# Attention stage of a decoder layer: transpositions at the head of a period, stream units dealt by estimated work

## The chip, the cores and the metric

The kernel runs on one core of one Trainium2 chip. The metric is the device time of one execution in microseconds (us): the median of 3 runs before the change is 1649.64 us (1649.29 to 1649.93). Beside these runs one execution was taken with the hardware profiler. Engines: PE is the matrix engine (PEld its weight loads), DVE the vector engine, ACT the activation engine, POOL the general-purpose vector engine, SP the engine that issues most DMAs.

## The reference

One layer over 512 positions and 2048 channels. Only the attention part matters here; the sentences below say where it stands.

```python
h = rms_norm(x, norm_g[l])
proj = h @ w_in[l]
q, kv, g_logits, z_a, uv, z_b, merge_logits = jnp.split(proj, SPLIT_IDX, axis=-1)
...
ss = jnp.einsum('bqgrd,bgqnkd->bgrqnk', qb, ks).astype(jnp.float32) * scale
...
p_s = jax.nn.softmax(ss.reshape(b, A_KV_GROUPS, A_REP, Q_BLOCK, n_top * SEL_BLOCK), axis=-1)
...
o_s = jnp.einsum('bgrqnk,bgqnkd->bqgrd', p_s.astype(vs.dtype), vs)
...
p_w = jax.nn.softmax(sw, axis=-1)
o_w = jnp.einsum('bgrqk,bkgd->bqgrd', p_w.astype(vwb.dtype), vwb)
o = (gb[:, :, 0, :, :, None] * o_c + gb[:, :, 1, :, :, None] * o_s +
     gb[:, :, 2, :, :, None] * o_w)
```

There are 16 heads of 64 channels in 4 groups, and three branches: a compressed one (o_c, 31 block keys), a selected one (o_s, where all 8 blocks of 64 keys are among the 16 to select, so that it is causal attention) and a window of 512 keys (o_w). Their outputs are gated, summed, and multiplied by SiLU of z_a. The other parts are a chunked gating unit, two up-projections, an output projection and a gated embedding, with the weight matrices read once.

## The kernel before

**The stream.** Every large matrix product is a job in one list (add_job), and a generator, gemm (line 170), works through it. A raw weight tile comes by DMA from SP, ACT casts its high part (hi, line 98), DVE subtracts to get the low part (lo, line 104), and PE multiplies in three matmuls of 512 columns (act_h by hi, act_l by hi, act_h by lo; lines 190 to 192). One `yield` of the generator after such a triple is a **unit**. A cast and a subtraction of 128x512 serve four units; they are issued two to three such tiles ahead (split_to). fill(n) takes n units. At the end of a job its evacuation runs: evac_q (line 277) makes two 64x512 casts and two subtractions of a scaled q tile qs, evac_za (line 292) a tanh and a gating multiply.

**The attention stage** runs while the stream goes through the jobs z0 q2 q3 z1 q4 q5 z2 q6 q7 z3 z4 z5 z6 z7 (za and q of pairs of heads), 16 units each, 224 in all; 19 are taken before its loop. The stage has 48 **slots** (line 748): for each of 8 pairs of heads ft, six slots (ft, i, br), with query block i = 3, 3, 2, 2, 1, 0 and one branch (selected or window) in the first four, both in the last two. A slot goes through four steps:

- scores (line 751): for two heads, two matmuls each of the query block with (i+1) x 128 keys (times branches) into a bank ps_s; DVE adds the position bias and takes the minimum while it moves the result to a tile prob (line 767). The exponentials on ACT (line 776) are issued two flushes later.
- weigh (line 781): DVE takes the reciprocal of the sums (line 785), multiplies by the gates (787) and scales prob (791).
- transpose_probs (line 806), for one block of at most two key blocks: 4 (or 2) transpositions on PE into a bank ps_t, a cast pth on ACT at once, and a subtraction ptl on DVE that is **deferred**.
- values (line 822), for one block: matmuls of pth and ptl with the values into ps_o; with the last block of a 256-column half, fold (line 839) adds two heads' rows through ACT, DVE and POOL.

The compressed branch has six steps of its own (cmp_keys to cmp_values), which run once for each group or pair; their matmuls use the ps_s banks too.

**The order.** All engines run their instructions in the order in which the program issues them. A deferred operation is issued at the next flush (line 90): before each step that uses PE, and in gemm before each new weight tile and at a job's end. The tags "s" and "t" have two PSUM banks each. The loop from line 929 goes through 51 **periods**. Period s issues scores of slot s, weigh of slot s-1, the first transposed block of slot s-2, the first values of slot s-3, then steps of the compressed branch, then the second blocks. Each period gets the same number of units, (224 - 19) / 51 = 4.02, spread evenly behind its steps on PE; weigh, cmp_weigh and cmp_keys (off_pe) get none.

Of the kernel before, what the change touches and what calls it, by code (L numbers as in the profile page):

```python
# [12 lines left out]
F32 = mybir.dt.float32  # L13
F32R = mybir.dt.float32r
# [6 lines left out]
P = 128  # L21
S = 512
# [29 lines left out]
def kernel(ctx: ExitStack, tc: tile.TileContext, x, p, norm_g, w_in,  # L52
# [15 lines left out]
    def bank(kind, name):  # L68
        return psum.tile([P, 512], F32, tag=kind, name=name)
# [20 lines left out]
    def flush():  # L90
        todo = list(deferred)
        deferred.clear()
        for f in todo:
            f()
# [14 lines left out]
    def split(hi, lo, src, scale=None, later=False):  # L109

        high(hi, src, scale)
        if later:
            deferred.append(lambda: low(hi, lo, src, scale))
        else:
            low(hi, lo, src, scale)
# [116 lines left out]
    def fill(n):  # L232
        for _ in range(n):
            next(run, None)

    def finish(name):
        while name not in done:
            next(run)
        flush()
# [10 lines left out]
    def kk(b, g):  # L250
        return g * 2 + b
# [123 lines left out]
    phase_b_units = 16 * 14  # L375
# [178 lines left out]
    with tc.tile_pool(name="xin", bufs=4, side="right") as xin:  # L554
# [43 lines left out]
        for j in range(2):  # L598
            b = bank("t", "ps_p")
# [6 lines left out]
        b = bank("o", "ps_g")  # L606
# [60 lines left out]
    with tc.tile_pool(name="cmp", bufs=1) as cmp:  # L667
# [17 lines left out]
        for n in range(2):  # L685
            b = bank("t", "ps_pe")
# [40 lines left out]
        b = bank("o", "ps_kc")  # L727
        nc.tensor.matmul(b[:, :128], w2t[lo_r].rearrange("e i f -> e (i f)"), h[lo_r, :, 0], start=True, stop=True)
        split(kc_h, kc_l, b[:, :128].rearrange("p (g n) -> p g n", g=GROUPS))
        b = bank("o", "ps_vc")  # L730
# [8 lines left out]
    att = ph_b.enter_context(tc.tile_pool(name="att", bufs=1))  # L739
# [6 lines left out]
    slots = []  # L746
    for ft in range(8):
        slots += [(ft, 3, (0,)), (ft, 3, (1,)), (ft, 2, (0,)), (ft, 2, (1,)), (ft, 1, (0, 1)), (ft, 0, (0, 1))]
    prob, obank, oc_t, pct_t = {}, {}, {}, {}

    def scores(s):
        ft, i, br = slots[s]
        finish(f"q{ft}")
        g, n = ft // 2, (i + 1) * P
        st = att.tile([P, 2, 2, 2], F32, tag="st", name="st", bufs=6)
        pts = []
        for hh in range(2):
            h = 2 * ft + hh
            b = bank("s", "ps_s")
            q = qs[h][:, i * P:i * P + P]  # L760
            o = b[:, :len(br) * n].rearrange("p (b n) -> p b n", b=len(br))
            s0 = kk(br[0], g)
            nc.tensor.matmul(o, q, ob_h[:, s0:s0 + len(br), :n], start=True, stop=False)
            nc.tensor.matmul(o, q, ob_l[:, s0:s0 + len(br), :n], start=False, stop=True)  # L764
            pt = att.tile([P, S], F32, tag="prob", name="prob", bufs=6)
            for j in range(len(br)):
                nc.vector.tensor_tensor_reduce(  # L767
                    out=pt[:, j * n:j * n + n], in0=o[:, j], in1=b0[:, 512 - n:], scale=-SLOPE[h], scalar=3.0e38,
                    op0=ALU.add, op1=ALU.min, accum_out=st[:, 0, j, hh:hh + 1])
            pts.append(pt)  # L770

        def exps():
            for hh in range(2):
                for j in range(len(br)):
                    sl = pts[hh][:, j * n:j * n + n]
                    nc.scalar.activation(sl, sl, AF.Exp, bias=st[:, 0, j, hh:hh + 1], scale=-1.0,  # L776
                                         accum_out=st[:, 1, j, hh:hh + 1])
        deferred.append(lambda: deferred.append(exps))
        prob[s] = (pts, st)
# [13 lines left out]
    def blocks(s):  # L793
        ft, i, br = slots[s]
        if i == 0:
            return [[(0, 0), (1, 0)]]
        res = []
        for j in range(len(br)):
            ks = list(range(i + 1))
            for a in range(0, len(ks), 2):  # L800
                res.append([(j, k) for k in ks[a:a + 2]])
        return res
# [3 lines left out]
    def transpose_probs(s, bi):  # L806
        ft, i, br = slots[s]
        n = (i + 1) * P
        pts, _ = prob[s]
        bl = blocks(s)[bi]  # L810
        b = bank("t", "ps_t")
        for e, (j, k) in enumerate(bl):
            for hh in range(2):
                c = j * n + k * P
                nc.tensor.transpose(b[:, (2 * e + hh) * P:(2 * e + hh + 1) * P], pts[hh][:, c:c + P], ident)  # L815
        w = 256 * len(bl)
        hi = att.tile([P, S], F32R, tag="pth", name="pth", bufs=3)
        lo = att.tile([P, S], F32R, tag="ptl", name="ptl", bufs=3)
        split(hi[:, :w], lo[:, :w], b[:, :w], later=True)
        moved[s, bi] = (hi, lo)  # L820

# [99 lines left out]
    off_pe = (cmp_keys, cmp_weigh, weigh)  # L921
    cmp_keys(0)
    for f, u in zip((cmp_scores, cmp_softmax, cmp_weigh, cmp_transpose), (4, 3, 4, 8)):
        fill(u)
        flush()
        f(0)
    n = len(slots)
    credit, per_period = 0.0, (phase_b_units - 19) / (n + 3)
    for s in range(n + 3):
        events = []  # L930
        if s < n:
            ft, j = slots[s][0], s % 6
            events.append((scores, s))
        if 1 <= s <= n:
            events.append((weigh, s - 1))
        tq = [(transpose_probs, s - 2, bi) for bi in range(len(blocks(s - 2)))] if 2 <= s <= n + 1 else []
        vq = [(values, s - 3, bi) for bi in range(len(blocks(s - 3)))] if s >= 3 else []
        events += tq[:1] + vq[:1]
        if s < n:
            if ft % 2 == 1 and ft < 7 and j == 3:  # L940
                events.append((cmp_keys, (ft + 1) // 2))
            if ft % 2 == 1 and ft < 7 and j == 5:
                events.append((cmp_scores, (ft + 1) // 2))
            if ft % 2 == 0 and ft > 0 and j in (1, 2, 4):
                events.append(({1: cmp_softmax, 2: cmp_weigh, 4: cmp_transpose}[j], ft // 2))
            if j == (3 if ft % 2 else 5):
                events.append((cmp_values, ft))
        events += tq[1:] + vq[1:]
        share = per_period / sum(e[0] not in off_pe for e in events)
        for e in events:  # L950
            if e[0] not in off_pe:
                flush()
            e[0](*e[1:])
            if e[0] not in off_pe:
                credit += share
                fill(int(credit))
                credit -= int(credit)
    finish("za7")
    flush()
    ph_ab.close()  # L960
# [7 lines left out]
    with tc.tile_pool(name="mlp", bufs=1) as mlp:  # L968
# [12 lines left out]
        for hf in range(2):  # L981
            b = bank("o", "ps_w")
# [7 lines left out]
        with tc.tile_pool(name="uzp", bufs=1) as uzp:  # L990
# [36 lines left out]
            for g in range(8):  # L1027
# [3 lines left out]
                for gg in ((0, 1, 2) if g == 2 else (g,)):  # L1031
                    b = bank("st"[gg % 2], "ps_sv")
# [75 lines left out]
```

## Time and profile before

| What | Number |
|---|---|
| median of 3 runs | 1649.64 us (1649.29 to 1649.93) |
| the profiled execution's own time | 1649.7 us |
| its span, first to last instruction | 1648.0 us |
| PE busy in the span | 1634.8 us, 99% |
| DVE, ACT, POOL busy in the span | 748.7, 616.5, 114.6 us |
| mean granted clock of PE | 0.998 |
| transpositions into ps_t, first and last start | 229.2 and 483.3 us |
| values into ps_o, first and last start | 234.0 and 487.5 us |

The profile has a page for the whole span, and views of parts of it. Busy time is the union of an engine's instructions. Matmuls overlap in a pipeline: one of 512 columns is recorded as 0.39 us long, but the next starts 0.23 us after it, so the starts show what a matmul costs. In a view in order of time, a row has the start (us from the span's start), the length, engine, line, operation, output and inputs with their shape, and the number of instructions merged in it; in brackets stands the engine's idle time ahead of it and what ended it. In the view of waits a row has who waited for whom, the sum in us, how often, and the longest. In the chain of waits a row has start, step and name.

### The profile page before, as it was taken

How to read it: one execution, taken by the hardware profiler on the slowest of the kernel's cores; microseconds unless marked ns; L12 is line 12 of the kernel's file. 1: busy time of each engine (PE TensorE's matmuls, PEld its weight loads, DVE VectorE, ACT ScalarE, POOL GpSimd, SP SyncE). 2: the span in 40 equal slices, each digit the busy share in tenths (PEclk: the TensorE clock that was granted, in tenths of full speed). 3: DMA queues.
4: the chain of work that ended last, by engine and by line, in shares of the span. 5: the costliest groups of instructions: out<-in, count | busy, mean ns of one | idle time of the engine just before them, and what ended most of it. 6: DMA issues, size and time to landing. Idle time of an engine off the chain costs nothing.

```text
span 1648.0 us, 20570 instructions
## 1 busy us (share of the span) xinstructions
PE 1634.8 (99%) x7821; PEld 1368.2 (83%) x7821; DVE 748.7 (45%) x1500; ACT 616.5 (37%) x1241; POOL 114.6 (7%) x145
## 2 busy tenths in 40 slices
PE   9999999999999999999999999999999999999997
PEld 8889988888888888888888888888888888888886
DVE  6544378988873363343322222223223433333335
ACT  6433356666653232233222222222223322223335
POOL 1200000110120001000000000000000000000001
PEclk9999999999999999999999999999999999999999
DMA  8422421122124333343333333333333533363333
GB/s 318 128 80 72 118 64 47 44 52 52 41 63 145 99 90 90 90 102 94 98 102 90 103 92 101 97 95 102 90 102 91 203 90 93 100 217 95 98 102 128
DMA packets 217202, 168.02 MB, mean 102 GB/s; under 512 B 4992, under 2 KB 190992, under 8 KB 215568
## 3 DMA queue, kind: packets, MB, share of 16 engines
q1 hardware_dynamic: 213488, 151.57, 32.9%
q0 software_dynamic: 3472, 14.79, 2.4%
q8 instruction: 61, 1.00, 0.3%
q10 hardware_dynamic: 144, 0.36, 0.1%
q14 instruction: 37, 0.30, 0.1%
HBM read 158.31 MB, written 8.39 MB: 101 GB/s over the span
## 4 chain that ended last, share of the span: by engine, by line
PE 96%; DVE 2%; ACT 1%; issue 0%; POOL 0%; DVEq 0%; POOLq 0%; ACTq 0%
PE ps_wo L202 4%; PE ps_ma L192 4%; PE ps_mb L192 4%; PE ps_mb L191 4%; PE ps_ma L191 4%; PE ps_mb L190 4%; PE ps_ma L190 4%; PE ps_wo L203 4%; PE ps_wo L204 4%; PE ps_pg L204 3%; PE ps_pg L202 3%; PE ps_pg L203 3%; PE ps_za L190 2%; PE ps_za L192 2%; PE ps_t L815 2%; PE ps_za L191 2%
## 5 line engine op out<-in xcount | busy, mean ns | idle before, releaser
L104 DVE TENSOR_TENSOR lo<-raw,hi 128x512 fp32r<-128x512 f32 (+1 forms) x536 | 366.9, 688 | 651.9 <-PE ps_mb L192 127.4
L98 ACT CAST hi<-raw 128x512 fp32r<-128x512 f32 (+1 forms) x536 | 328.2, 615 | 732.4 <-PE ps_wo L204 105.9
L202 PE MATMUL ps_wo<-hi,act_h 128*128 128x512 f32 x256 | 100.2, 392 | 0.1
L204 PE MATMUL ps_wo<-hi,act_l 128*128 128x512 f32 x256 | 99.6, 389 | 0.0
L203 PE MATMUL ps_wo<-lo,act_h 128*128 128x512 f32 x256 | 99.6, 389 | 0.0
L190 PE MATMUL ps_ma<-act_h,hi 128*128 128x512 f32 x256 | 99.6, 389 | 0.0
L191 PE MATMUL ps_ma<-act_l,hi 128*128 128x512 f32 x256 | 99.6, 389 | 0.0
L192 PE MATMUL ps_ma<-act_h,lo 128*128 128x512 f32 x256 | 99.6, 389 | 0.0
L190 PE MATMUL ps_mb<-act_h,hi 128*128 128x512 f32 x256 | 99.6, 389 | 0.0
L191 PE MATMUL ps_mb<-act_l,hi 128*128 128x512 f32 x256 | 99.6, 389 | 0.0
L192 PE MATMUL ps_mb<-act_h,lo 128*128 128x512 f32 x256 | 99.6, 389 | 0.0
L98 ACT CAST pth<-ps_t 128x512 fp32r<-128x512 f32 (+1 forms) x88 | 47.9, 544 | 65.7 <-PE ps_t L815 65.4
L776 ACT ACTIVATE prob<-prob,st 128x512 f32<-128x512 f32 (+3 forms) x128 | 70.7, 555 | 4.0 <-DVE st L767 3.8
L452 POOL TENSOR_TENSOR m<-sig,sig 128x512 f32<-128x512 f32 x16 | 27.0, 1686 | 582.3 <-DVE sig L450 464.2
L104 DVE TENSOR_TENSOR ptl<-ps_t,pth 128x512 fp32r<-128x512 f32 (+1 forms) x88 | 56.3, 639 | 21.1 <-ACT pth L98 20.2
L767 DVE CUSTOM_DVE_ANT_0 prob<-ps_s,b 128x512 f32<-128x512 f32 (+3 forms) x128 | 56.3, 486 | 10.1 <-PE ps_s L764 9.9
L202 PEld LDWEIGHTS ps_wo<-hi,act_h 128*128 128x128 f32 x256 | 48.1, 188 | 10.3 <-DVE sig L450 0.5
L191 PEld LDWEIGHTS ps_ma<-act_l,hi 128*128 128x128 f32 x256 | 48.0, 188 | 10.0
L191 PEld LDWEIGHTS ps_mb<-act_l,hi 128*128 128x128 f32 x256 | 48.0, 188 | 10.0
L204 PEld LDWEIGHTS ps_wo<-hi,act_l 128*128 128x128 f32 x256 | 48.0, 188 | 10.0
L190 PEld LDWEIGHTS ps_ma<-act_h,hi 128*128 128x128 f32 x256 | 48.0, 188 | 10.0
L190 PEld LDWEIGHTS ps_mb<-act_h,hi 128*128 128x128 f32 x256 | 48.0, 188 | 10.0
(311 smaller groups left out, 3684.6 us busy)
## 6 DMA issues: line engine op xcount, KB each, us to landing
raw<-in_w_in_dram SPq DMA_DIRECT2D x164, 512.0 KB, 3.7
raw<-in_w_out_dram SPq DMA_DIRECT2D x32, 512.0 KB, 3.6
raw<-in_w_ple_gate_dram SPq DMA_DIRECT2D x32, 512.0 KB, 3.6
raw<-in_w_up_a_dram SPq DMA_DIRECT2D x16, 512.0 KB, 3.8
raw<-in_w_up_b_dram SPq DMA_DIRECT2D x16, 512.0 KB, 3.7
xt<-in_x_dram SPq DMA_DIRECT2D x4, 1024.0 KB, 9.5
spill<-ple POOLq DMA_DIRECT2D x4, 1024.0 KB, 8.2
m<-in_x_dram POOLq DMA_DIRECT2D x4, 1024.0 KB, 7.8
```

Source lines behind the costliest of these rows:

```text
L98: nc.scalar.copy(hi, src)
L104: nc.vector.tensor_tensor(out=lo, in0=src, in1=hi.bitcast(F32), op=ALU.subtract)
L190: nc.tensor.matmul(ps, hi[:, j], ah, start=st, stop=False)
L191: nc.tensor.matmul(ps, hi[:, j], al, start=False, stop=False)
L192: nc.tensor.matmul(ps, lo[:, j], ah, start=False, stop=sp)
L202: nc.tensor.matmul(o, ah[:, sl], hi[:, j], start=st, stop=False)
L203: nc.tensor.matmul(o, ah[:, sl], lo[:, j], start=False, stop=False)
L204: nc.tensor.matmul(o, al[:, sl], hi[:, j], start=False, stop=sp)
L452: nc.gpsimd.tensor_tensor(out=merge_tiles["m"][:, f], in0=merge_tiles[0], in1=t, op=ALU.add)
L767: nc.vector.tensor_tensor_reduce(out=pt[:, j * n:j * n + n], in0=o[:, j], in1=b0[:, 512 - n:], scale=-SLOPE[h], scalar=3.0e38, op0=ALU.add ...
L776: nc.scalar.activation(sl, sl, AF.Exp, bias=st[:, 0, j, hh:hh + 1], scale=-1.0, accum_out=st[:, 1, j, hh:hh + 1])
L815: nc.tensor.transpose(b[:, (2 * e + hh) * P:(2 * e + hh + 1) * P], pts[hh][:, c:c + P], ident)
```

## The change

The transposed blocks of slot s-2 are issued together, as the first step of period s (transpose_slot); the values of slot s-3 stay behind scores and weigh. Since now up to four transposed blocks are alive and only two slots of prob, pth and ptl get a fourth buffer and prob goes from six to four.

The units are no longer dealt evenly: a function cost gives each step an estimated time on PE and on DVE. Half of the units is dealt evenly over the periods; the other half so that the estimated ratio of DVE to PE time, with 0.24 us on DVE and 0.68 us on PE for a unit, is the same in each period. Within a period they are spread evenly behind the steps on PE, as before.

```diff
-            pt = att.tile([P, S], F32, tag="prob", name="prob", bufs=6)
+            pt = att.tile([P, S], F32, tag="prob", name="prob", bufs=4)
...
-        hi = att.tile([P, S], F32R, tag="pth", name="pth", bufs=3)
-        lo = att.tile([P, S], F32R, tag="ptl", name="ptl", bufs=3)
+        hi = att.tile([P, S], F32R, tag="pth", name="pth", bufs=4)
+        lo = att.tile([P, S], F32R, tag="ptl", name="ptl", bufs=4)
...
+    def transpose_slot(s):
+        for bi in range(len(blocks(s))):
+            transpose_probs(s, bi)
+
+    def cost(e):
+
+        f, a = e[0], e[1]
+        if f in (scores, weigh, transpose_slot, values):
+            ft, i, br = slots[a]
+            n, w = (i + 1) * P, [256 * len(b) for b in blocks(a)]
+        if f is scores:
+            return 4 * (len(br) * n / 2400 + 0.014), 2 * len(br) * (0.1 + n / 960)
+        if f is weigh:
+            return 0.0, 0.45 + 2 * (0.1 + len(br) * n / 1800)
+        if f is transpose_slot:
+            return 0.09 + sum(w) / 128 * 0.109, sum(0.08 + v / 960 for v in w)
+        if f is values:
+            last = i % 2 == 0 and br[-1] == 1 and e[2] == len(w) - 1
+            return w[e[2]] / 256 * 0.24, 1.5 * last
+        return {cmp_keys: (0.0, 0.3), cmp_scores: (1.85, 0.0), cmp_softmax: (0.55, 2.1), cmp_weigh: (0.0, 1.6),
+                cmp_transpose: (0.55, 0.8), cmp_values: (1.1, 0.0)}[f]
+
     n = len(slots)
-    credit, per_period = 0.0, (phase_b_units - 19) / (n + 3)
+    periods = []
     for s in range(n + 3):
         events = []
+        if 2 <= s <= n + 1:
+            events.append((transpose_slot, s - 2))
         if s < n:
             ft, j = slots[s][0], s % 6
             events.append((scores, s))
         if 1 <= s <= n:
             events.append((weigh, s - 1))
-        tq = [(transpose_probs, s - 2, bi) for bi in range(len(blocks(s - 2)))] if 2 <= s <= n + 1 else []
         vq = [(values, s - 3, bi) for bi in range(len(blocks(s - 3)))] if s >= 3 else []
-        events += tq[:1] + vq[:1]
+        events += vq[:1]
...
-        events += tq[1:] + vq[1:]
-        share = per_period / sum(e[0] not in off_pe for e in events)
+        events += vq[1:]
+        periods.append(events)
+    units = phase_b_units - 19
+    work = [[sum(cost(e)[i] for e in events) for i in range(2)] for events in periods]
+    pe, dve = (sum(w[i] for w in work) for i in range(2))
+    ratio = (dve + 0.24 * units) / (pe + 0.68 * units)
+    credit = 0.0
+    for events, (pe, dve) in zip(periods, work):
+        share = 0.5 * units / len(periods) + 0.5 * (dve - ratio * pe) / (0.68 * ratio - 0.24)
+        share /= sum(e[0] not in off_pe for e in events)
         for e in events:
             if e[0] not in off_pe:
                 flush()
             e[0](*e[1:])
             if e[0] not in off_pe:
                 credit += share
-                fill(int(credit))
-                credit -= int(credit)
+                if credit >= 1:
+                    fill(int(credit))
+                    credit -= int(credit)
```

## The prediction

> **What bounds the kernel now.** I read the page's head and its chain of waits first, then the waits and busy times of the attention stage alone, then the order of time inside it.
>
> ```profile
> span 1648.0 us, 20570 instructions
> PE 96%; DVE 2%; ACT 1%; issue 0%; POOL 0%; DVEq 0%; POOLq 0%; ACTq 0%
> ```
>
> The chain that ends last is TensorE (PE) work for 96% of the span. Every part outside the attention stage keeps its instructions and their order, so only the stage from 215 to 490 us can change.
>
> ```profile
> 215.00:490.00 275.00, 273.31 (x1532) 230.57 (x1531) 231.70 (x693) 178.20 (x480) 33.88 (x60) 1.00 0.19 51
> ```
>
> The columns are the stretch, its length, then busy time and count of PE, PEld, DVE, ACT and POOL, clock, DMA share, GB/s. PE is busy for 273.31 of 275 us at full clock, DVE for 231.70. The change removes and adds no PE instruction, so the stage can only lose the time in which PE stands still. How much is that?
>
> ```profile
> PEld ps_t L815 <- DVE ptl L104: 2.8, 4, 1.7
> PE ps_t L815 <- DVE ptl L104: 1.2, 1, 1.2
> ```
>
> ```profile
> 302.93 1.39 DVE L106 SCALAR_TENSOR_TENSOR qs<-ps_q,qs 64x512 fp32r<-64x512 f32 x2
> 304.35 0.69 DVE L104 TENSOR_TENSOR ptl<-ps_t,pth 128x512 fp32r<-128x512 f32 x1
> ...
> 305.10 0.66 PE L815 MATMUL ps_t<-ident,prob 128*128 128x128 f32 x4 [1.24 <-DVE ptl L104]
> ```
>
> Transpositions wait four times for a bank of ps_t, 2.8 us by the weight loads. The longest shows why: DVE is behind, the two subtractions of a new q tile (1.39 us) stand ahead of the ptl that frees the bank. The other bound is PE's idle time in the stage, 275 - 273.31 = 1.7 us. I take 2.3 us, the middle, as **all that the change can win**, 0.14% of the span.
>
> **The change, part by part.** In period s the old order is scores(s), weigh(s-1), first block of transpositions of slot s-2, values of slot s-3, second block, with 4 stream units spread among them. The new order puts both blocks of slot s-2 first. Prices on PE, from the chain of waits around 310 us (start, step, name):
>
> ```profile
> 310.14 0.12 PE ps_s L763
> ...
> 311.07 0.23 PE ps_q L192
> 311.30 0.44 PE ps_t L815 x4
> 311.74 0.12 PE ps_o L834
> ...
> 312.90 0.86 PE ps_c L916 x2
> ```
>
> A matmul of 512 columns steps 0.23, so a unit (3) is 0.69 and a scores step (4) 0.93 at 512 columns, 0.70 at 384, 0.47 at 256 in all (a slot of i=0). Four transpositions are 0.44, a block's values 0.48 (4 x 0.12), cmp_values 0.86, cmp_scores 8 x 0.23 = 1.86.
>
> Would merging eight transpositions save a switch? A block of two shows that there is none to save:
>
> ```profile
> 240.65 0.38 PE L815 MATMUL ps_t<-ident,prob 128*128 128x128 f32 x2
> 240.78 0.48 PE L190 MATMUL ps_q<-act_h,hi 128*128 128x512 f32 x1
> 241.10 0.40 PE L191 MATMUL ps_q<-act_l,hi 128*128 128x512 f32 x1
> ```
>
> 0.13 until the next start, and 0.32 instead of 0.23 after it: 0.22, half of 0.44. Merged or not, 0.11 each: **nothing**.
>
> The buffer counts cost nothing. With 4 prob tiles scores(s) overwrites those of slot s-2, whose transpositions stand ahead of the scores matmuls on PE itself; were that cover gone, DVE would wait until the 0.87 us of transpositions end, which is earlier than it comes to them (2.5, below). With 4 pth and ptl the fill of slot s-2 overwrites slot s-4, whose values ran in the period before. No DMA is added; loads follow the units as before, at a DMA share of 0.19.
>
> What the order does cost is **a loop that goes round once a period**. T(s-2) reads prob after weigh(s-2), which was issued in period s-1, on DVE behind the evacuation of scores(s-1), which stands behind the two ptl of T(s-3), which wait for ACT's pth, which waits for T(s-3) at that period's start. Before, T came after scores(s) and some units, so the same weigh had a whole period. The loop's prices:
>
> ```profile
> 229.16 0.60 PE L815 MATMUL ps_t<-ident,prob 128*128 128x128 f32 x4
> ...
> 229.79 0.59 ACT L98 CAST pth<-ps_t 128x512 fp32r<-128x512 f32 x1 [2.03 <-PE ps_t L815]
> ...
> 230.45 0.68 DVE L104 TENSOR_TENSOR ptl<-ps_t,pth 128x512 fp32r<-128x512 f32 x1
> ...
> 231.05 0.68 DVE L104 TENSOR_TENSOR lo<-raw,hi 128x512 fp32r<-128x512 f32 x1
> ```
>
> From T's start to the first ptl 230.45 - 229.16 = 1.29; each further DVE subtraction steps 0.60 (a block of 256 columns I take at 0.33, in proportion). So DVE is through both ptl at 2.49 (slots of i=3 and i=1), 2.22 (i=2) or 1.89 (i=0, one block).
>
> ```profile
> 294.32 0.55 DVE L767 CUSTOM_DVE_ANT_0 prob<-ps_s,b 128x384 f32<-128x384 f32 x1
> ...
> 295.27 0.16 DVE L785 RECIPROCAL st<-st 128x2 f32<-128x2 f32 x1
> ...
> 295.66 0.88 DVE L791 TENSOR_SCALAR prob<-prob,st 128x512 f32<-128x512 f32 x2
> ...
> 306.16 0.41 DVE L767 CUSTOM_DVE_ANT_0 prob<-ps_s,b 128x256 f32<-128x256 f32 x1
> ...
> 307.53 0.16 DVE L785 RECIPROCAL st<-st 128x2 f32<-128x2 f32 x1
> ...
> 307.92 0.75 DVE L791 TENSOR_SCALAR prob<-prob,st 128x384 f32<-128x384 f32 x2
> ...
> 310.42 0.29 DVE L767 CUSTOM_DVE_ANT_0 prob<-ps_s,b 128x128 f32<-128x128 f32 x1
> ...
> 311.27 0.17 DVE L785 RECIPROCAL st<-st 128x4 f32<-128x4 f32 x1
> ...
> 311.67 1.14 DVE L791 TENSOR_SCALAR prob<-prob,st 128x256 f32<-128x256 f32 x4
> ...
> 316.11 0.69 DVE L767 CUSTOM_DVE_ANT_0 prob<-ps_s,b 128x512 f32<-128x512 f32 x1 [0.43 <-PE ps_s L764]
> ...
> 317.34 0.17 DVE L785 RECIPROCAL st<-st 128x4 f32<-128x4 f32 x1
> ...
> 317.75 0.88 DVE L791 TENSOR_SCALAR prob<-prob,st 128x128 f32<-128x128 f32 x4
> ```
>
> Evacuating scores (first L767 to L785): i=3 1.23, i=2 0.95, i=1 1.37, i=0 0.85. Weighing (L785 to the end of L791): i=3 1.27, i=2 1.14, i=1 1.54, i=0 1.29. Weigh to transposition I take as 0.06.
>
> The dealing comes from cost(): summed over the stage 132.1 on PE and 197.5 on DVE give a ratio of (197.5 + 0.24 x 205) / (132.1 + 0.68 x 205) = 0.909; a period gets 205/51/2 = 2.01 units and half of (dve - 0.909 pe) / 0.378. The result is 2 to 8 units: 2 where cmp_values or cmp_scores load PE, 8 with cmp_weigh, mostly 3 or 4 in the periods 3 and 4 after a multiple of 6. Each fourth unit carries a lo (0.60 on DVE); dealt ahead of weigh, it lies in the loop.
>
> Worked for period 10 (3 units: one after T, one after scores, one after the first values). PE: six transpositions 0.65 + scores 0.93 + values 0.96 + 3 x 0.69 = 4.61. Loop: 2.22 + lo 0.60 + evacuation 1.37 + weigh of an i=2 slot 1.14 + 0.06 = 5.39. T(9) starts **0.78 late**, and PE with it. The same sum for each of the periods 2 to 47 leaves these short by over half a us: 2 (1.41), 10 (0.78), 15 (0.64), 19 (2.04: q5 ends there ahead of weigh, adding the 1.39 above), 41 (0.78), 43 (0.65), 46 (1.47), together 7.8; in period 46 za6's gate adds
>
> ```profile
> 345.23 0.68 DVE L304 SCALAR_TENSOR_TENSOR zt<-zt,ps_za 128x512 f32<-128x512 f32 x1
> ```
>
> Six more are short by 0.04 to 0.28, together 0.8. The other periods have up to 1.8 us to spare, which nothing can carry over.
>
> A second wait is of the same kind. cmp_values and cmp_scores take the ps_s bank that the first head of scores(s) has just filled. DVE reads it after the ptl: in period 9 at 2.49 + 0.47 + 0.06 = 3.02 is done, when PE stands there at 0.87 + 0.70 + 0.69 + 0.48 = 2.74: 0.28 short. By this sum four periods lose 0.42 each (5, 11, 23, 41), three 0.28 (9, 33, 45), one 0.19 (21), one 1.02 (35, a lo between): 3.7.
>
> Shortages in full: 7.8 + 0.8 + 3.7 = 12.3. If each loop is really 0.5 us shorter than my rows make it, 7 x 0.5 less of 7.8 and one of the second kind remain: 4.3 + 0.5 = 4.8. I take the middle, 8.6, since the errors (ACT late for its cast, DVE still at leftovers; reads that overlap) go both ways. **Sum: 8.6 - 2.3 = +6.3 us.** The profiled execution took 1649.7 us, 1.7 outside its span; 1649.7 + 6.3 = 1656.0. The median of the runs is 1649.64, no other number.
>
> POOL can stretch the loop:
>
> ```profile
> 346.06 1.46 POOL L306 TENSOR_TENSOR o<-o,zt 128x256 f32<-128x256 f32 x2 [13.03 <-DVE zt L304]
> ...
> 346.82 1.25 DVE L104 TENSOR_TENSOR lo<-raw,hi 128x512 fp32r<-128x512 f32 x1
> ```
>
> A lo that fell under POOL's two multiplies took 1.25 instead of 0.68. The Trainium skill, page "SBUF — State Buffer", section "SBUF: two separate sides", says that DVE and GpSimd hold one pair of ports as an exclusive lock, so that the later one waits outright; the trace agrees with 0.57 us. Were each lo in the seven loops above caught so, the sum would be 7 x 0.57 = 4.0 higher; the lock is held for only 33.88 of 275 us, so I leave it out of the sum.
>
> **Rivals.** (a) *The dealing wins and the loop never binds.* DVE keeps up in every period, the four bank waits go. For it: before, each period got 4 units whatever work DVE had in it; now those with softmax, folds or weighing of the compressed branch get 5 to 8. Against it: the sums above, where light periods fall below the loop even with DVE idle at their start. It decides if casts and ptl run so early that the loop stays under 4.4 us, the shortest period. Time 1649.7 - 2.3 = 1647.4 to no change, 1649.7. (b) *The leftovers pile up.* ACT runs the compressed softmax's exponentials, which wait for three DVE passes, ahead of the next T's casts, and fold and POOL work falls into the loops; then the shortages count in full or more: 12.3 - 2.3 = +10.0, 1659.7, and with 4 us more 1663.7. For it: DVE's 84% here; against: periods with softmax have over 1 us to spare. (c) *The change does nothing to the order that counts*: PE's instructions are the same and DVE's lag sets all: inside (a).
>
> **How the numbers follow.** Forecast 0.43 (own range 1652.2 to 1659.7: 4.8 or 12.3, less 2.3), (a) 0.40, (b) 0.17. About 0.2%, 3.3 us, is what a measurement of this kernel can tell from no change. (a) cannot win more than 2.3 by these rows, so faster by over 0.2% is left 0.04 for something not seen; all of (b) and nearly all of the forecast are slower by over that, 0.58; same 0.38. The range runs from 1647.5, nearly all of (a), to 1661.0, which leaves out the upper part of (b).
>
> **What would show it.** Right: in the stage, waits of ps_t for DVE's weigh (prob L791) of 4 to 9 us in all, the longest around the q5 job and za6; ps_c or its loads waiting for L767; the waits on ptl gone; PE idle of 5 us and more. If merged transpositions cost other than 0.11 each, the second step is wrong. The prediction fails if ps_t waits for L791 less than 2 us in all, or if stalls appear at scores or values instead.

## The result, and the profile after

The changed kernel takes **1677.29 us** (median of 5 runs, 1675.97 to 1677.46) against 1649.64 us: 1.0166 of the time before, 95% interval 1.0151 to 1.0181. It is slower by 27.6 us, where the forecast had 6.3 and the range ended at 1661.0.

The page of the profile after, the lines that answer to those of before:

```profile
span 1675.7 us, 20668 instructions
...
PE 91%; DVE 5%; ACT 2%; issue 1%; DVEq 0%; POOL 0%; ACTq 0%; POOLq 0%
```

The chain that ends last now runs through DVE and ACT for 7% of the span instead of 3%. The attention stage, by busy times (columns as before):

```profile
215.00:520.00 305.00, 285.29 (x1542) 237.12 (x1541) 231.88 (x695) 183.30 (x483) 37.12 (x60) 0.99 0.17 46
```

DVE has the same 231.9 us of work as before (231.7). PE stands idle for 305 - 285.29 = 19.7 us, where it was 1.7 in 275 us, and its mean clock is 0.99. The last values matmul starts at 516.0 us instead of 487.5; behind it the two kernels run alike, within 0.8 us. Who waits, in the same stretch:

```profile
PE ps_t L815 <- DVE prob L791: 13.8, 12, 2.6
PEld ps_t L815 <- issue: 13.1, 10, 3.0
PEld ps_t L815 <- DVE prob L791: 8.0, 13, 2.6
...
PEld ps_c L916 <- issue: 3.6, 5, 1.1
...
PEld ps_c L867 <- issue: 2.9, 3, 1.6
...
PE ps_c L916 <- DVE st L767: 2.8, 6, 0.9
...
PE ps_c L867 <- DVE st L767: 2.3, 3, 1.5
```

The matmul's rows and the weight load's rows tell the same waits twice, and waits shorter than a matmul's tail hardly show, so the sums come better from the starts: for each slot's transpositions, how much later they start than the step of the matmul ahead of them allows, plus the gaps above 0.11 us inside the group. Summed over the 48 slots this is **20.6 us**; the same for the compressed branch's matmuls gives 3.8 (cmp_values) and 2.8 (cmp_scores), **6.6 us**. The four waits for ptl of the kernel before are gone; the prediction's 2.3 us stands for them here. 20.6 + 6.6 - 2.3 = 24.9; by their steps 1.5 and 0.9 us more lie in matmuls that ran slowly after two long waits (last section), which makes about 27.3 of the 27.6.

The period that the prediction worked through shows that its prices were good. Period 10 of the changed kernel, PE and DVE in order of time:

```profile
273.69 0.82 PE L815 MATMUL ps_t<-ident,prob 128*128 128x128 f32 x6
...
278.21 0.28 PE L835 MATMUL ps_o<-ptl,vt 128*128 128x256 f32 x1
278.88 0.57 PE L815 MATMUL ps_t<-ident,prob 128*128 128x128 f32 x2 [0.38 <-DVE prob L791]
```

```profile
275.00 1.02 DVE L104 TENSOR_TENSOR ptl<-ps_t,pth 128x512 fp32r<-128x512 f32 x2 [2.03 <-ACT pth L98]
275.94 0.68 DVE L104 TENSOR_TENSOR lo<-raw,hi 128x512 fp32r<-128x512 f32 x1
276.54 0.42 DVE L767 CUSTOM_DVE_ANT_0 prob<-ps_s,b 128x256 f32<-128x256 f32 x1
...
278.31 0.75 DVE L791 TENSOR_SCALAR prob<-prob,st 128x384 f32<-128x384 f32 x2
```

The first ptl comes 1.31 us after T (1.29 forecast), the loop is 278.88 - 273.69 = 5.19 us (5.39), and T(9), the transpositions of slot 9, is 0.73 us late with its inner gap of 0.19 (0.78). Period 15 shows what the forecast had not:

```profile
304.10 0.88 DVE L791 TENSOR_SCALAR prob<-prob,st 128x512 f32<-128x512 f32 x2
304.90 0.41 DVE L850 TENSOR_TENSOR fold<-fold,ps_o 64x256 f32<-64x256 f32 x1
305.33 0.42 DVE L851 TENSOR_TENSOR fold<-fold,ps_o 64x256 f32<-64x256 f32 x1
305.78 0.69 DVE L896 TENSOR_REDUCE cst<-cs 128x16 f32<-128x512 f32 x1
306.50 0.25 DVE L897 RECIPROCAL cst<-cst 128x16 f32<-128x16 f32 x1
306.79 0.69 DVE L898 TENSOR_TENSOR cst<-cst,gates 128x16 f32<-128x16 f32 x1
307.52 1.39 DVE L106 SCALAR_TENSOR_TENSOR qs<-ps_q,qs 64x512 fp32r<-64x512 f32 x2
308.94 1.29 DVE L104 TENSOR_TENSOR ptl<-ps_t,pth 128x512 fp32r<-128x512 f32 x2
```

```profile
305.30 1.03 PE L815 MATMUL ps_t<-ident,prob 128*128 128x128 f32 x8
...
306.72 1.08 ACT L98 CAST pth<-ps_t 128x512 fp32r<-128x512 f32 x2
...
309.66 0.40 PE L192 MATMUL ps_q<-act_h,lo 128*128 128x512 f32 x1
312.65 1.00 PE L815 MATMUL ps_t<-ident,prob 128*128 128x128 f32 x6 [2.60 <-DVE prob L791]
```

T(13) starts at 305.30, so its first ptl could start at 306.61. DVE comes to it at 308.94, 2.3 us later: behind the weigh of the period before it still had the fold, the compressed branch's weighing and a q tile in its queue. (ACT was late as well: its cast pth started 1.42 us after T instead of the 0.63 of the forecast's rows, so that part of the delay would have stayed without DVE's queue.) The whole loop moves by that, and T(14) starts 312.65 - 309.66 - 0.23 = 2.76 us late, where the forecast had 0.64.

### The profile page after: what moved, and what is told of

The parts are those of the page before. It is cut to its first block, busy times and chain, and to the rows that moved or that the text cites. A ratio compares the mean times of both kernels' runs of the same rounds, so it can differ in the third digit from the quotient of the medians.

```text
span 1675.7 us, 20668 instructions
## 1 busy us (share of the span) xinstructions
PE 1644.5 (98%) x7821; PEld 1372.9 (82%) x7821; DVE 748.2 (45%) x1500; ACT 620.7 (37%) x1241; POOL 117.1 (7%) x145
## 4 chain that ended last, share of the span: by engine, by line
PE 91%; DVE 5%; ACT 2%; issue 1%; DVEq 0%; POOL 0%; ACTq 0%; POOLq 0%
PE ps_wo L202 3%; PE ps_ma L190 3%; PE ps_mb L190 3%; PE ps_mb L192 3%; PE ps_ma L192 3%; PE ps_mb L191 3%; PE ps_ma L191 3%; PE ps_wo L203 3%; PE ps_wo L204 3%; PE ps_pg L204 3%; PE ps_pg L202 3%; PE ps_pg L203 3%; PE ps_u L190 2%; PE ps_u L191 2%; PE ps_zb L191 2%; PE ps_vn L203 2%
## 5 line engine op out<-in xcount | busy, mean ns | idle before, releaser
L104 DVE TENSOR_TENSOR ptl<-ps_t,pth 128x512 fp32r<-128x512 f32 (+1 forms) x88 | 52.9, 639 | 43.9 <-ACT pth L98 43.6
L815 PE MATMUL ps_t<-ident,prob 128*128 128x128 f32 x320 | 47.1, 280 | 14.2 <-DVE prob L791 13.8
L815 PEld LDWEIGHTS ps_t<-ident,prob 128*128 128x128 f32 x320 | 37.5, 142 | 25.4 <-issue 13.1
L192 PEld LDWEIGHTS ps_ma<-act_h,lo 128*128 128x128 f32 x256 | 48.1, 188 | 10.0
L192 PEld LDWEIGHTS ps_mb<-act_h,lo 128*128 128x128 f32 x256 | 48.1, 188 | 10.0
```

What stands on the lines that cost most here:

```text
L104: nc.vector.tensor_tensor(out=lo, in0=src, in1=hi.bitcast(F32), op=ALU.subtract)
L192: nc.tensor.matmul(ps, lo[:, j], ah, start=False, stop=sp)
```

## Experiments

**Order alone and dealing alone.** order_only keeps the new order and deals evenly; deal_only keeps the old order and buffers and deals by half the work.

```diff
 order_only
-        share = 0.5 * units / len(periods) + 0.5 * (dve - ratio * pe) / (0.68 * ratio - 0.24)
+        share = units / len(periods)
 deal_only
-        if 2 <= s <= n + 1:
-            events.append((transpose_slot, s - 2))
...
+        tq = [(transpose_probs, s - 2, bi) for bi in range(len(blocks(s - 2)))] if 2 <= s <= n + 1 else []
...
-        events += vq[:1]
+        events += tq[:1] + vq[:1]
...
-        events += vq[1:]
+        events += tq[1:] + vq[1:]
```

> The new order and buffers, with the old even dealing of 4.02 units a period. Theory L (the loop: a slot's transpositions at the head of a period wait for a weigh that stands on DVE behind the evacuation of scores and two ptl): the stalls stay or grow, since folds and the compressed branch's work now fall into periods of 4 units too; 1670 to 1690 us, waits of ps_t for weigh of 15 us and more. Rival D (the uneven dealing is what hurts, by its periods of 2 or 3 units): within 5 us of the 1649.6 before.

> The old order and buffers (blocks of transpositions apart, behind scores and weigh), with the new dealing by half the estimated work. L: no loop, so no stall of more than some tenths: 1647 to 1651 us, at best 2.3 us under the 1649.6 before. D: most of the 27 us loss comes with it, 1665 us or more.

order_only: 1676.75 us (1676.15 to 1677.44), ratio 1.0163 [1.0146, 1.0180]. deal_only: 1648.88 us (1648.36 to 1649.23), ratio 0.9994 [0.9985, 1.0004]. The order brings the whole loss, the dealing none of it. (The buffer counts changed together with the order and were not varied alone; no view of waits, here or in the changed kernel, names one of those buffers.) By the starts, the waits of transpositions in order_only are 27.2 us, more than in the changed kernel, and those of the compressed branch about 1; the new dealing moves waits between the two but does not cure the order.

**Merged, but later.** Both blocks of a slot in one go, behind scores, weigh and the first values; six prob and three pth and ptl tiles as before the change, as in deal_only.

```diff
-        if 2 <= s <= n + 1:
-            events.append((transpose_slot, s - 2))
...
         events += vq[:1]
+        if 2 <= s <= n + 1:
+            events.append((transpose_slot, s - 2))
```

> The new dealing, and both transposed blocks of a slot in one go, but behind scores, weigh and the first values of the period; buffers as before the change. L: the same weigh now has some 2 to 3 us more, so the waits of ps_t for weigh go and the time is 1647 to 1653 us. Rival M (eight transpositions in a row hurt by themselves, through the two ps_t banks and the casts that come in one burst): above 1660 us.

1650.16 us (1649.82 to 1650.60), ratio 1.0003 [0.9994, 1.0012]. The waits of transpositions come to less than 0.01 us in all 48 slots. Eight transpositions in a row cost nothing by themselves; their place at the head of the period does. Some of the values now wait for ptl; by the weight loads that is the small price of this place:

```profile
PEld ps_o L835 <- DVE ptl L104: 2.0, 5, 0.5
```

**Weigh first.** Behind the transpositions DVE weighs slot s-1 before it evacuates the scores of slot s. The exponentials that weigh needs are issued ahead of it by flushes.

```diff
         if 2 <= s <= n + 1:
             events.append((transpose_slot, s - 2))
+        if 1 <= s <= n:
+            events.append((weigh, s - 1))
...
-        if 1 <= s <= n:
-            events.append((weigh, s - 1))
```

> The changed kernel with weigh(s-1) issued ahead of scores(s), right behind the transpositions, so that DVE weighs before it evacuates the period's scores. L: the transpositions' wait for weigh goes (20 us of the loss), the compressed branch's wait for its ps_s bank stays (6 us) or grows a little, since weigh may stand ahead of the evacuation: 1650 to 1662 us. M and D: as the changed kernel, 1670 us or more.

1698.29 us (1696.77 to 1700.34), ratio 1.0295 [1.0280, 1.0310]: a miss, and instructive. Its waits (L921, L872, L911 and L881 are cmp_values, cmp_scores, cmp_transpose and cmp_softmax, L820 and L796 the transpositions and weigh; the lines are shifted by the edit):

```profile
PE ps_c L921 <- DVE st L767: 13.5, 6, 3.4
DVE st L790 <- ACT prob L777: 13.4, 21, 1.1
...
PE ps_c L872 <- DVE st L767: 5.7, 3, 3.0
...
PE ps_t L820 <- DVE prob L796: 4.2, 3, 3.4
...
PE ps_c L911 <- DVE st L767: 3.7, 2, 2.5
...
PE ps_c L881 <- DVE st L767: 3.6, 2, 2.3
```

The transpositions' waits did shrink, by the starts to 8.6 us. But DVE now stood at weigh until ACT had the exponentials (13.4 us in 21 waits), and the evacuation of the scores behind it came later, so that every step of the compressed branch waited for its bank: 28.7 us by the starts of its first matmuls (14.6 + 6.2 + 4.0 + 3.9). The wait had only changed its consumer, and DVE's own idle time was added. The rest of the loss is clock: behind these waits PE ran at a granted clock of 0.50 in eight stretches of the attention stage, 30.7 us in all (last section); by the steps of the matmuls in them this is worth some 14 us.

**The parts of the loop.** Three edits of the changed kernel: the ptl of a slot issued behind the next scores; the compressed branch's steps behind both values; the compressed branch's weighing left out.

```diff
 ptl_after_scores
-        split(hi[:, :w], lo[:, :w], b[:, :w], later=True)
+        high(hi[:, :w], b[:, :w])
+        late.append(lambda: low(hi[:, :w], lo[:, :w], b[:, :w]))
...
             e[0](*e[1:])
+            while late and e[0] is not transpose_slot:
+                late.popleft()()
 cmp_last
-        events += vq[:1]
+        events += vq
...
-        events += vq[1:]
 no_cmp_weigh
     def cmp_weigh(g):
+        if g:
+            return
```

> The changed kernel with the two ptl of a slot issued behind the evacuation of the next scores instead of ahead of it. Theory Q (DVE works through its queue in order, so a waiting matmul waits for all that stands ahead of its releaser): the compressed branch's wait for its ps_s bank goes, some 5 to 6 us; the loop keeps the same sum, since weigh still stands behind both, so the transpositions' waits stay at 15 to 25 us; 1667 to 1675 us. Rival P (ptl, which waits for ACT's cast, is the link that makes the loop too long): both kinds of wait go, 1650 to 1658 us.

> The changed kernel with the compressed branch's steps behind both blocks of values instead of between them. Q: these steps come 0.5 us and a unit later, so their 6.6 us of waiting for a bank go down to 2 us or less; PE is then earlier at the next transpositions, where four of nine such periods have no room, so that 1 to 2 us of it come back there: 1672 to 1675 us. Rival (the waits only stand in place of each other): no change, 1677 us.

> The changed kernel without the weighing of the compressed branch in groups 1 to 3 (three DVE and two POOL operations a group are left out). Theory C (what DVE still has in its queue at a period's start is carried into the next loop): the waits of T(14), T(26) and T(38), 2.95, 2.26 and 1.30 us with what follows them inside the group, fall to under 1 us each, and the time by 4 to 6 us to 1671 to 1673 us. Rival (each period starts afresh, as the forecast had it): within 1 us of the changed kernel's 1677.

ptl_after_scores: 1678.77 us (1676.87 to 1681.29), ratio 1.0178 [1.0164, 1.0192]. The bank waits of the compressed branch fall from 6.6 to 0.3 us, those of the transpositions rise from 20.6 to 27.9, and the time lies above the range that was expected. So ptl is no special link: what stands ahead of weigh on DVE makes the loop, in whatever order, and PE, no longer held up in the middle of a period, waits at its end.

cmp_last: 1672.69 us (1670.39 to 1673.15), ratio 1.0137 [1.0123, 1.0151]. The bank waits fall to 1.1 us, the transpositions' rise to 23.2: of 5.5 us won, 2.6 come back, a little more than expected.

no_cmp_weigh: 1671.76 us (1671.03 to 1674.03), ratio 1.0139 [1.0123, 1.0154], 5.5 us less than the changed kernel. The waits of T(14), T(26) and T(38) go from 2.95, 2.26 and 1.30 to 2.15, 1.16 and 0.22 us: less than hoped, but what is left has its row. Period 15 of this kernel on DVE:

```profile
305.21 0.42 DVE L851 TENSOR_TENSOR fold<-fold,ps_o 64x256 f32<-64x256 f32 x1
306.61 1.39 DVE L106 SCALAR_TENSOR_TENSOR qs<-ps_q,qs 64x512 fp32r<-64x512 f32 x2 [0.97 <-ACT qs L100]
308.03 1.29 DVE L104 TENSOR_TENSOR ptl<-ps_t,pth 128x512 fp32r<-128x512 f32 x2
```

Without the weighing DVE stands 0.97 us for ACT's cast of the q tile and then does the q tile ahead of ptl, which starts at 308.03 instead of 308.94. T(26) and T(38) fall by 1.10 and 1.08 us; the three DVE operations that are left out took 0.68 + 0.25 + 0.18 = 1.11 us there. In all, the transpositions' waits fall from 20.6 to 16.9 us. Most of the rest is clock: the profiled execution, at 1671.17 us, has neither of the two slow stretches.

**How much to deal by work.** The old order with the whole of the units dealt by work, with a quarter, and half once more.

```diff
 deal_full
-        share = 0.5 * units / len(periods) + 0.5 * (dve - ratio * pe) / (0.68 * ratio - 0.24)
+        share = (dve - ratio * pe) / (0.68 * ratio - 0.24)
 deal_quarter
+        share = 0.75 * units / len(periods) + 0.25 * (dve - ratio * pe) / (0.68 * ratio - 0.24)
```

> The old order with the units dealt wholly by estimated work instead of half. If DVE's lag is what is left of the stalls, it takes the rest of them: 1647.5 to 1649 us, against 1648.9 with half. If the estimate is too coarse, light periods run dry of units and stall: 1650 us and more.

> The old order with a quarter of the units dealt by estimated work. If the stalls left in the old order come from DVE's lag in heavy periods, it lies between even dealing and half: 1648.5 to 1649.5 us; if the best weight is under a half, it is the fastest: 1647.5 to 1648.5 us.

> The old order with half the units dealt by estimated work once more, with more rounds, to tell whether it beats the kernel before: 1648.4 to 1649.2 us, 0.4 to 1.2 us under the kernel before, if the first runs hold; within 0.3 us of it if not.

deal_full: 1653.98 us (1653.80 to 1654.69), ratio 1.0027 [1.0016, 1.0038]. Its waits:

```profile
PE ps_c L867 <- DVE st L767: 1.8, 2, 1.2
...
PE ps_c L916 <- POOL o L854: 1.3, 1, 1.3
...
PE ps_t L815 <- DVE ptl L104: 0.8, 1, 0.8
```

Where cmp_scores or cmp_values stand in a period that was left with hardly any unit, they come to a bank or a tile that is not ready. deal_quarter: 1648.54 us (1648.29 to 1648.88), ratio 0.9993 [0.9984, 1.0002]. deal_half_again: 1648.80 us (1648.59 to 1649.46), ratio 0.9995 [0.9986, 1.0003], beside 21 runs of the kernel before with a median of 1649.78 (1649.32 to 1650.39). Quarter and half are the fastest kernels here, by 1.0 to 1.2 us in the medians; the intervals just take in no change.

## Why the prediction was wrong

- **What bounds the kernel, and the most that could be won: held.** The dealing alone, in the old order, was 0.8 to 1.2 us faster in the medians, of the 2.3 that were there, with intervals that just take in no change.
- **Merged transpositions cost nothing: held** (merged_mid, no waits). No view of waits names one of the changed buffers.
- **The loop: the right mechanism.** Waits of ps_t for weigh appear where none were, and they go when the order goes (deal_only, merged_mid). Its rows were right to some 0.2 us (period 10). Of the seven late transpositions that were named by over half a us, six came: 1.41, 0.78, 0.64, 2.04, 0.65 and 1.47 were forecast after the periods 2, 10, 15, 19, 43 and 46, and 1.32, 0.73, 2.95, 3.31, 0.61 and 1.49 measured; after period 41 it was 0.21 instead of 0.78. T(1), T(9), T(42) and T(45) fit to 0.1 us; T(14) and T(18), after the periods 15 and 19, do not.
- **The step that failed is the first term of the loop, "From T's start to the first ptl 230.45 - 229.16 = 1.29", which was taken for the same in every period.** It let DVE be free, 1.29 us after T, at the head of each period, but for a q tile in period 19 and za6's gate in period 46. Room to spare is indeed not carried over from period to period; work left in a queue is. What DVE has behind weigh (folds 0.83 us, the compressed branch's weighing, 1.7 in period 15, a q tile 1.39, a lo) stands ahead of the next ptl, and with a q tile DVE also waits there for ACT's cast. In the loops ahead of T(3), T(7), T(14), T(26), T(30), T(37) and T(38) the first ptl came 2.85 to 4.25 us after T. These seven were 11.0 us late together; the forecast had named only T(14), with 0.64. No_cmp_weigh shows the carrying by taking one such leftover away; for the q tiles, folds and lo the rows show it, and no run took them away. T(0), whose period the sum left out, was 1.45 late. T(18) was 3.31 late instead of 2.04 for another reason: its loop's first ptl came in time, at 1.31, but then DVE stood 0.56 us for ACT's cast of the q tile, and some 0.6 us of it is the slow clock (2.68 in cmp_last, at full clock). With all this the transpositions' part of the full sum, 7.8 + 0.8 = 8.6, was 20.6.
- **POOL** was left out of the sum. In the loop ahead of T(14) it counted once: the multiply into cst took 0.69 us under a POOL multiply, where it took 0.18 ahead of T(26).
- **Halving the sum: wrong, by itself.** The full sum, 12.3, was cut to 8.6 because errors were said to go both ways. Here they went nearly all one way (T(40), 0.21 instead of 0.78, is the exception): a late queue adds to a wait, an early one only leaves room that is lost. But even the full sum gives 1659.7 and not 1677.29. The bank waits too were 6.6, not 3.7 or less.
- **Rival (b), leftovers piling up, was what happened**, and had 0.17; its price, 1659.7 to 1663.7, took the shortages in full and 4 us more, and not the carried work, so the time is far above it too. (a) is refuted: the loop binds with either dealing. (c) falls with it.

The slow clock after long waits, 2.4 us, was not forecast at all; some 0.3 us of the 27.6 is not assigned.

## What to carry to other kernels

Moving a step to the head of a period shortens the time that its producer has by the steps it was moved past: write down the loop from the step through every queue back to itself, and put into it what each in-order engine still has in its queue at that point, not only what belongs to the loop. When a full sum of shortages comes out, do not halve it for luck, since slack is lost and lateness adds. And a wait in an in-order queue that is cured by moving the producer forward turns up at whatever was moved back (weigh_first); a step placed a little later, with the producer's whole period ahead of it, paid only some 2 us, at its own consumer (merged_mid).

## What the runs showed of the hardware that was not expected

After the two longest waits of the profiled execution PE ran at a granted clock of 0.50, for 3.41 us each time. Stretches of the changed kernel (busy times as before, then clock, DMA share and GB/s), the waits of 2.76, 2.34 and 2.08 us end in the first, third and fifth:

```profile
310.79:314.20 3.41, 1.55 (x10) 1.32 (x11) 2.03 (x10) 1.97 (x6) 0.00 (x0) 1.00 0.00 0
314.21:317.62 3.41, 3.41 (x11) 2.73 (x10) 3.21 (x13) 2.60 (x9) 0.00 (x0) 0.50 0.02 5
334.69:338.10 3.41, 1.17 (x7) 0.51 (x5) 3.23 (x10) 1.52 (x4) 0.00 (x0) 1.00 0.01 2
338.10:341.51 3.41, 3.41 (x12) 3.02 (x13) 1.38 (x2) 1.17 (x2) 0.00 (x0) 0.50 0.00 0
385.89:389.30 3.41, 1.59 (x9) 1.04 (x7) 3.27 (x12) 1.22 (x5) 2.38 (x6) 1.00 0.00 0
389.30:392.71 3.41, 3.31 (x19) 2.89 (x20) 2.70 (x9) 1.88 (x6) 0.00 (x0) 1.00 0.40 91
```

The clock is 0.50 in the second and fourth stretch, and the matmuls step 0.42 us instead of 0.23 (rows below); after 2.08 us of waiting it stays at 1.00.

```profile
314.60 0.63 PE L764 MATMUL ps_s<-ob_l,qs 128*128 128x512 f32 x1
315.02 0.63 PE L763 MATMUL ps_s<-ob_h,qs 128*128 128x512 f32 x1
315.45 0.63 PE L764 MATMUL ps_s<-ob_l,qs 128*128 128x512 f32 x1
```

It is not the length of the wait alone: in cmp_last the same three transpositions waited 2.55, 2.34 and 2.07 us and the clock stayed at 1.00 in its profiled execution,

```profile
308.94:312.35 3.41, 1.62 (x10) 1.40 (x11) 2.03 (x9) 2.05 (x7) 0.00 (x0) 1.00 0.00 0
312.35:315.76 3.41, 3.41 (x21) 2.91 (x20) 3.34 (x14) 2.71 (x10) 0.00 (x0) 1.00 0.01 5
332.83:336.24 3.41, 1.95 (x12) 1.64 (x13) 2.02 (x6) 1.87 (x6) 0.00 (x0) 1.00 0.00 0
336.24:339.65 3.41, 3.41 (x20) 2.98 (x19) 3.12 (x10) 2.07 (x7) 0.00 (x0) 1.00 0.00 0
380.62:384.03 3.41, 1.54 (x9) 1.02 (x7) 3.27 (x12) 1.28 (x5) 2.37 (x6) 1.00 0.00 0
384.03:387.44 3.41, 3.37 (x19) 2.91 (x20) 2.70 (x9) 1.88 (x6) 0.00 (x0) 1.00 0.44 116
```

which took 1670.39 us at a mean clock of 0.999, while its three other runs, at 0.996 to 0.997, took 1672.46 to 1673.15.

The stretches in these views are not chosen freely. In each trace's record of the clock the changes of the clock in the attention stage lie whole multiples of 3.41 us after its first change in the execution, so time falls into a grid of such stretches, and a wait can lie in one of them or across a border. What tells the two cases apart is how long PE was busy within one: in the 12 traces there are 14 full-clock stretches with a slow one behind them, with PE busy for 0.60 to 1.55 us of 3.41; of the others between 200 and 560 us none has under 1.54, so that the bound lies near 1.55 in these rows. The Trainium skill, page "TensorE: Matmul & The Clock Gate", section "Part 1: The HAM clock gate (the "warmup" mystery)", tells of a clock of half rate after an idle window of some 3.4 us. Half rate agrees with the 0.50 here; but PE was busy for up to 1.55 us of the stretch ahead, and the wait was as short as 2.3 us, so for the length the measurement decides. So a wait of over 2 us can cost PE its clock on top, some 1 to 2 us each time in this kernel, and not in every run, since it depends on where in the grid it falls.
